# Input laid out feature-major by the host, row norms as column sums of squares, first weights in four loads

## The chip, the cores and the metric

The kernel runs on one core of a Trainium2 chip. The metric is the device time of one execution in microseconds (us), as the median of several runs. A core has a matrix engine (TensorE, in the profile PE for matmuls and PEld for weight loads), a vector engine (VectorE, DVE), an activation engine (ScalarE, ACT), a general engine (GpSimd, POOL) and SyncE (SP), which here only issues DMAs. Each engine works through its own instructions in order and waits on semaphores for the others. DMAs are issued from SP's queue and, a few, from ACT's.

## The reference

Two layers of a diffusion trunk: 512 latent tokens and 256 context tokens of width 1024, all in float32. Layer 0 is differential attention, layer 1 grouped-query attention. Only the beginning of layer 0 matters here:

```python
def rms_norm(x, g):
    y = xf * lax.rsqrt(jnp.mean(xf * xf, axis=-1, keepdims=True) + NORM_EPS)
    return (y * g).astype(x.dtype)
...
    shift, scale, gate = split(silu(c) @ ada_w[i] + ada_b[i], 3)
    cshift, cscale, cgate = split(silu(c_ctx) @ ada_w[i] + ada_b[i], 3)
    h  = rms_norm(x,  pre_g[i]) * (1.0 + scale)  + shift
    hc = rms_norm(xc, pre_g[i]) * (1.0 + cscale) + cshift
    p = h @ a_w_in        # q, k, v, z; the same weights for hc
```

So h, the input of the first projections, needs the norm of each token's row and a shift and a scale for each of 1024 features. The shift and scale weights of layer 0 are 1024 x 2048 floats, 8.4 MB, for two vectors c and c_ctx.

## The kernel before

Everything is kept feature-major: a tile of 128 features (feature tile kt, 0 to 7) lies on the 128 partitions and the tokens lie along the free dimension, 512 latent ones and then 256 context ones (768). A float32 product is made of three float32r matmuls: each operand is split in a high part (`whi`, `h` from a cast on ACT) and a low part (`wlo`, the second `h`, from a subtraction on DVE or POOL), and `mm3` (lines 146 to 148) multiplies high by high, high by low and low by high.

The opening stage of layer 0, the first 50 us or so, does this:

- `x_load` (L551) brings the tokens in six tiles of 128 tokens x 1024 features, rows of 4 KB, four of x first and two of the context later.
- `x_tile` squares each tile on ACT with a sum (L571), makes 1/norm on POOL (`rstd_of`, L382 and L383), scales the tile (L217, on DVE, one on POOL), transposes it on PE in eight 128x128 pieces (L577) and copies the result to `xnt`, 128 features x 8 x 768 tokens (L582 on ACT, L584 on DVE).
- `ada_load8` (L489) and `ada_load` (L475) bring the shift/scale weights as they lie in the layer's matrix: feature tiles 0 and 1 each as a first small group in runs of 512 bytes, then three groups of two feature tiles in runs of 1 KB. I number these five groups first to fifth. `ada_pe` multiplies them with silu(c) in four column strips (`cols4`, L465), `ada_red` copies the row to SBUF (L496), turns it into columns (L500) and adds the biases (`mods_set`, L510 to L512): `mods` holds shift and scale.
- `ht` makes h for one feature tile, latent or context: hf = xnt * scale + shift (L602), cast (L603), low part (L604).
- `w_load` and `v_load` (L527, L532) bring the first head's q and k weights in two halves and its v weights in two tiles; `w_split` and `v_split` (L539 to L545) split them.
- `qk_part` and `v_part` are the projections by `mm3`: q and k of head 0 into `sc`, v of heads 0 and 1 into the `bk` banks, feature tile by feature tile as h becomes available.

The code is written once, in program order with priorities (`tc.high_priority`, offsets in `PRI`); a scheduler puts the instructions of each engine in order ahead of the run from its own model of the time. The tables `EXS`, `EHF`, `EHL`, `EWL`, `EVL` choose DVE ('v'), POOL ('p') or ACT ('a') for single steps. The DMAs of one queue start in the order written; a DMA waits, on SP, for its buffer and for the DMA eight places before it.

```python
    row = pj(256)
    run(ada_pe(ca, row))
    w_split(0, raw_qk)
    row_b = pj(256)
    ada_red(0, 1, row)
    run(ada_pe(cb, row_b))
    ht(0, 0)
```

Of the kernel before, what the change touches and what calls it, by code (L numbers as in the profile page):

```python
# [9 lines left out]
F32 = mybir.dt.float32  # L10
F32R = mybir.dt.float32r
AF = mybir.ActivationFunctionType
ALU = mybir.AluOpType
# [3 lines left out]
P = 128  # L17
D = 1024
KT = 8
S = 512  # L20
C = 256
T = 768
NT = 6
NQ = 4
# [14 lines left out]
AGB = 11  # L39
# [9 lines left out]
XE = [2, 2, 2, 2, 3, 3]  # L49
NWARM = 12  # L50
XLATE = 1
# [28 lines left out]
def f32(ap):  # L80
    return ap.bitcast(F32)
# [3 lines left out]
def tile_backbone(  # L85
    ctx: ExitStack,
    tc: tile.TileContext,
    x: bass.AP,
    xc: bass.AP,
    c_col: bass.AP,  # L90
    ada_w: bass.AP,
    ada_bT: bass.AP,
# [13 lines left out]
    nc = tc.nc  # L106
    uid = [0]

    def nm(s):
        uid[0] += 1  # L110
        return f"{s}_{uid[0]}"
# [8 lines left out]
    def small(n=1):  # L120
        return sm.tile([P, 8], F32, tag="sm", name=nm("sm"), bufs=24)[:, :n]
# [5 lines left out]
    def trp():  # L127
        i = lru.pop(0)
        lru.append(i)
        return banks[i]  # L130
# [10 lines left out]
    def sc2():  # L141
        scs.append(scs.pop(0))
        return scs[-1]
# [17 lines left out]
    eps = con.tile([P, 1], F32, name="eps")  # L161
# [5 lines left out]
        nc.tensor.matmul(banks[3][:, :P], ones, ones, start=True, stop=True)  # L167

    ccol = con.tile([P, 2, KT], F32, name="ccol")
    nc.sync.dma_start(ccol, c_col)  # L170
# [42 lines left out]
    def scaled(eng, dst, src, s_):  # L213
        if eng == "a":
            nc.scalar.activation(dst, src, AF.Copy, scale=s_)
        else:
            (nc.vector if eng == "v" else nc.gpsimd).tensor_scalar(dst, src, s_, 1.0, ALU.mult, ALU.mult)  # L217

    VP = {"v": nc.vector, "p": nc.gpsimd}
# [215 lines left out]
    hhi, hlo = [None] * KT, [None] * KT  # L435
# [29 lines left out]
                prev = nc.tensor.matmul(  # L465
                    o[32 * j:32 * j + 32, :], s32[:, 4 * g + j, :], ts[j], start=g == 0, stop=g == 1)

    ada_v = ada_w[0].rearrange("(k p) (w n) -> p k w n", p=P, w=3)
# [14 lines left out]

    def ada_load8(e):
        cs = []
        for k in (0, 4):
            g = st.tile([P, D], F32, tag="ag", name=nm("ag"), bufs=AGB).rearrange("p (k w n) -> p k w n", k=4, w=2)
            for w in range(2):
                nc.sync.dma_start(g[:, :, w], ada_v[:, k:k + 4, w, e * P:(e + 1) * P])  # L489
            cs += [g[:, j].rearrange("p w n -> p (w n)") for j in range(4)]  # L490
        return cs

    def ada_red(k0, nb, o):
# [20 lines left out]
    def raw_tile():  # L514
        return wp.tile([P, 1024], F32, tag="raw", name=nm("raw"), bufs=2)
# [4 lines left out]
    del ws.items[:4]  # L520
    ws.pools.append(ws.pools.pop(0))

    def w_load(half):
        r = raw_tile()
        sl = slice(half * 512, half * 512 + 512)
        for j in range(2):
            nc.sync.dma_start(r[:, j * 512:j * 512 + 512], a_w[j][:, sl])  # L527
        return r

    def v_load(half):  # L530
        rv = raw_tile()
        nc.sync.dma_start(rv, a_w[half * 4 + 2])  # L532
        return rv

    def w_split(half, r):
        sl = slice(half * 512, half * 512 + 512)
        for j, (hi, lo) in enumerate((wq, wk0)):
            rj = r[:, j * 512:j * 512 + 512]
            nc.scalar.copy(hi[:, sl], rj)  # L539
            VP[EWL[2 * half + j]].tensor_tensor(lo[:, sl], rj, f32(hi[:, sl]), ALU.subtract)  # L540

    def v_split(half, rv):
        hi, lo = wv0[half]
        nc.scalar.copy(hi, rv)
        VP[EVL[half]].tensor_tensor(lo, rv, f32(hi), ALU.subtract)  # L545

    xs = []

    def x_load(t):
        xt = st.tile([P, D], F32, tag="ag", name=nm("xt"), bufs=AGB)  # L550
        nc.sync.dma_start(xt, x[t * P:(t + 1) * P, :] if t < NQ else xc[(t - NQ) * P:(t - NQ + 1) * P, :])  # L551
        xs.append(xt)

    for t in range(NQ):
        x_load(t)
    ca = ada_load8(0)
    raw_qk = w_load(0)
    cb = ada_load8(1)
    raw_v = v_load(0)
    if XLATE < 1:  # L560
        x_load(4)
        x_load(5)
    nxt = ada_load(1)
    if XLATE:
        x_load(4)
        x_load(5)

    def x_tile(t):
        ssq = small()
        junk = st.tile([P, D], mybir.dt.bfloat16, tag="junk", name=nm("junk"), bufs=1)  # L570
        nc.scalar.activation(junk, xs[t], AF.Square, accum_out=ssq)  # L571
        r = rstd_of(ssq, D)
        scaled(EXS[t], xs[t], xs[t], r)
        pt = [sc2()] if t < NQ else [trp(), trp()]
        for kt in range(KT):
            o = pt[0][:, kt // 4, :] if t < NQ else pt[kt // 4]
            nc.tensor.transpose(o[:, (kt % 4) * P:(kt % 4 + 1) * P], xs[t][:, kt * P:(kt + 1) * P], ident)  # L577
        for j in range(2):
            src = (pt[0][:, j] if t < NQ else pt[j]).rearrange("p (k n) -> p k n", k=4)
            dst = xnt[:, 4 * j:4 * j + 4, t * P:(t + 1) * P]  # L580
            if XE[t] >> j & 1:
                nc.scalar.copy(dst, src)  # L582
            else:
                nc.vector.tensor_copy(dst, src)  # L584

    def pri(f, i):
        def g(*args):
            with tc.high_priority(offset=PRI[i]):
                f(*args)

        return g

    def ht(kt, v):
        if v == 0:
            hhi[kt], hlo[kt] = htile(), htile()
        a, b = ((0, 512), (512, 768))[v]
        hf = st.tile([P, 512], F32, tag="hf", name=nm("hf"), bufs=2)[:, :b - a]
        s_, h_ = mods[:, 0, v, 1, kt:kt + 1], mods[:, 0, v, 0, kt:kt + 1]
        if EHF[v][kt] == "a":
            nc.scalar.activation(hf, xnt[:, kt, a:b], AF.Identity, scale=s_, bias=h_)  # L600
        else:
            VP[EHF[v][kt]].tensor_scalar(hf, xnt[:, kt, a:b], s_, h_, ALU.mult, ALU.add)  # L602
        nc.scalar.copy(hhi[kt][:, a:b], hf)  # L603
        VP[EHL[v][kt]].tensor_tensor(hlo[kt][:, a:b], hf, f32(hhi[kt][:, a:b]), ALU.subtract)  # L604

    x_tile, ht, ada_red, w_split, v_split = pri(x_tile, 0), pri(ht, 1), pri(ada_red, 2), pri(w_split, 3), pri(v_split, 3)
    for t in range(NQ):
        x_tile(t)
    row = pj(256)
    run(ada_pe(ca, row))  # L610
    w_split(0, raw_qk)
    row_b = pj(256)
    ada_red(0, 1, row)
    run(ada_pe(cb, row_b))
# [43 lines left out]
    run(qk_part((0,), 0))  # L658
    ada_red(1, 1, row_b)
    ht(1, 0)  # L660
    v_split(0, raw_v)
    raw_qk = w_load(1)
    raw_v = v_load(1)
    ov = [pj(512) for _ in range(2)]
    for pr in range(NQT):
        kts = (2 * pr, 2 * pr + 1)
        if pr + 1 < NQT:
            cs = nxt
            if pr + 2 < NQT:
                nxt = ada_load(pr + 2)  # L670
            row = pj(512)
            ada = ada_pe(cs, row)
            if pr == 0:
                mix(ada, qk_part((1,), 0), v_part(kts, (0, 1, 2, 3)))
            else:
                mix(ada, qk_part(kts, 0), v_part(kts, (0, 1)))
            ada_red(2 * pr + 2, 2, row)
            if pr == 0:
                w_split(1, raw_qk)
            if pr == 1:  # L680
                v_split(1, raw_v)
# [920 lines left out]
    return ra, rb.reshape(P, 2, 512)  # L1602


# [57 lines left out]
```

## Time and profile before

| | |
|---|---|
| time, three runs | 838.15, 838.4, 839.8 us; median 838.4 |
| profiled execution | span 840.2 us from its first to its last instruction, the time that the profile gives for it |
| TensorE busy | 801.7 us of the span; 30.6 of the first 40 us |
| DMA | 77.78 MB over the span; 15.95 MB of it in the first 60 us |
| granted TensorE clock | 0.990 on average |

The profile is one execution; its span lies 1.8 us above the median of the runs. Rows of instructions give the start, the duration, the engine, the line of the kernel, the operation, what it writes and reads and its shape; in brackets stands how long the engine was idle before it and what ended that. Rows of groups give a count, the busy time, the mean duration in ns, and the idle time before with its releasers. An f32 matmul that isn't float32r shows as two records.

### The profile page before, as it was taken

The numbers are of one execution on the slowest core, as the hardware profiler recorded it, in microseconds if no ns is written. First come the engines' busy times: TensorE is split into PE (matmuls) and PEld (weight loads), VectorE is DVE, ScalarE is ACT, GpSimd is POOL, SyncE is SP. The second block draws the span as 40 slices with busy tenths as digits, with TensorE's granted clock in tenths as the row PEclk, the third lists the DMA queues.
The fourth block names the chain that finished last, engine by engine and source line by source line (L and its number), as shares of the span: only waits on it lengthen the run. The fifth ranks groups of instructions, "written<-read, shape, count | busy, mean of one in ns | idle before, by whom it ended". The sixth has DMA issues, their size and how long they took to land. (4 is left out here: it accounts for less than half of the span.)

```text
span 840.2 us, 14479 instructions
## 1 busy us (share of the span) xinstructions
PE 801.7 (95%) x5472; PEld 705.9 (84%) x5472; DVE 477.9 (57%) x897; ACT 459.0 (55%) x1001; POOL 452.8 (54%) x629
## 2 busy tenths in 40 slices
PE   7899999999999999999999999989998989899997
PEld 5578888888877898778988898779998889889986
DVE  4424467764858425675267843664266676665634
ACT  5424457664574644765457743754364656566731
POOL 4344676966476753776733312585776746624201
PEclk9999999999999999999999999999999999999999
DMA  9934211122133321314410051031232340300112
GB/s 300 352 109 126 88 39 35 67 83 82 63 114 116 122 77 63 137 52 151 126 51 26 27 200 51 26 108 51 77 101 76 86 162 4 101 26 26 53 48 101
DMA packets 41541, 77.78 MB, mean 93 GB/s; under 512 B 3584, under 2 KB 18688, under 8 KB 41472
## 3 DMA queue, kind: packets, MB, share of 16 engines
q1 hardware_dynamic: 38048, 71.71, 26.0%
q10 hardware_dynamic: 3424, 5.15, 1.8%
q8 instruction: 43, 0.70, 0.3%
q14 instruction: 26, 0.21, 0.1%
HBM read 70.56 MB, written 2.10 MB: 86 GB/s over the span
## 5 line engine op out<-in xcount | busy, mean ns | idle before, releaser
L146 PE MATMUL bk<-whi,h 128*128 128x256 f32 (+1 forms) x592 | 176.7, 301 | 6.5 <-ACT hf L1229 2.0
L203 POOL TENSOR_TENSOR wlo<-raw,whi 128x256 fp32r<-128x256 f32 x184 | 138.6, 784 | 70.3 <-ACT whi L209 69.3
L147 PE MATMUL bk<-wlo,h 128*128 128x256 f32 (+1 forms) x592 | 175.8, 298 | 0.3 <-DVE wlo L203 0.3
L148 PE MATMUL bk<-whi,h 128*128 128x256 f32 (+1 forms) x592 | 174.8, 298 | 0.8 <-DVE h L1232 0.8
L146 PE MATMUL bk<-h,whi 128*128 128x512 f32 (+2 forms) x416 | 147.1, 354 | 3.1 <-ACT sq L968 1.5
L147 PE MATMUL bk<-h,whi 128*128 128x512 f32 (+2 forms) x416 | 144.7, 348 | 0.0
L148 PE MATMUL bk<-h,wlo 128*128 128x512 f32 (+2 forms) x416 | 144.7, 348 | 0.1
L146 PEld LDWEIGHTS bk<-whi,h 128*128 128x128 f32 x592 | 112.0, 189 | 15.8 <-issue 3.6
L147 PEld LDWEIGHTS bk<-wlo,h 128*128 128x128 f32 x592 | 112.2, 189 | 4.8 <-issue 1.0
L148 PEld LDWEIGHTS bk<-whi,h 128*128 128x128 f32 x592 | 111.6, 189 | 4.8 <-DVE h L1232 1.2
L217 POOL TENSOR_SCALAR p<-p,sm 128x768 f32<-128x768 f32 (+1 forms) x80 | 67.7, 849 | 76.6 <-DVE sm L882 29.1
L146 PEld LDWEIGHTS bk<-h,whi 128*128 128x128 f32 x416 | 78.2, 188 | 17.8 <-issue 4.8
L209 ACT CAST whi<-raw 128x1024 fp32r<-128x1024 f32 x64 | 67.4, 1053 | 39.2 <-DMA raw<-in_b_w 12.3
L148 PEld LDWEIGHTS bk<-h,wlo 128*128 128x128 f32 x416 | 78.1, 188 | 8.6 <-issue 1.3
L147 PEld LDWEIGHTS bk<-h,whi 128*128 128x128 f32 x416 | 78.3, 188 | 6.5 <-issue 0.3
L879 ACT ACTIVATE p<-sc,sm 128x768 f32<-128x768 f32 (+1 forms) x68 | 59.9, 883 | 25.8 <-DVE sm L876 25.1
L876 DVE TENSOR_REDUCE sm<-sc 128x1 f32<-128x768 f32 (+1 forms) x68 | 60.6, 918 | 20.5 <-PE sc L871 20.5
L203 POOL TENSOR_TENSOR sz<-sz,za 128x192 f32<-128x192 f32 (+1 forms) x48 | 32.5, 697 | 41.2 <-ACT za L183 41.2
L939 ACT CAST ah<-bk 128x512 fp32r<-128x512 f32 x56 | 31.7, 592 | 34.4 <-PE bk L936 28.1
L887 DVE SCALAR_TENSOR_TENSOR p<-p,sm,p 128x768 f32<-128x768 f32 (+1 forms) x34 | 38.4, 1129 | 20.2 <-POOL p L217 19.0
L940 DVE TENSOR_TENSOR al<-bk,ah 128x512 fp32r<-128x512 f32 x56 | 37.6, 685 | 17.4 <-ACT ah L939 16.9
L871 PE MATMUL sc<-qk,qk 64*128 64x384 f32 (+1 forms) x396 | 46.8, 359 | 0.1
(247 smaller groups left out, 1720.2 us busy)
## 6 DMA issues: line engine op xcount, KB each, us to landing
raw<-in_a_w SPq DMA_DIRECT2D x30, 512.0 KB, 3.5
araw<-in_ada_w SPq DMA_DIRECT2D x12, 1024.0 KB, 5.1
raw<-in_b_w SPq DMA_DIRECT2D x20, 512.0 KB, 3.5
ag<-in_ada_w SPq DMA_DIRECT2D x32, 256.0 KB, 6.4
raw<-in_w_out SPq DMA_DIRECT2D x16, 512.0 KB, 3.4
sw<-qr ACTq DMA_DIRECT2D x32, 128.0 KB, 2.4
raw<-in_ada_w SPq DMA_DIRECT2D x8, 512.0 KB, 3.9
xt<-in_x SPq DMA_DIRECT2D x4, 512.0 KB, 5.4
```

Source lines behind the costliest of these rows:

```text
L146: nc.tensor.matmul(o, ahi, bhi, start=start, stop=False)
L147: nc.tensor.matmul(o, ahi, blo, start=False, stop=False)
L148: nc.tensor.matmul(o, alo, bhi, start=False, stop=stop)
L203: eng.tensor_tensor(dst[:, i:i + n], a[:, i:i + n], b[:, i:i + n], op)
L209: nc.scalar.copy(hi, r)
L217: (nc.vector if eng == "v" else nc.gpsimd).tensor_scalar(dst, src, s_, 1.0, ALU.mult, ALU.mult)
L871: prev = nc.tensor.matmul(sc[m][:, j if nk == T else m, :w], a[r, tok], b[r, c], start=i == 0, stop=i == 2)
L876: nc.vector.tensor_reduce(mx, scv, AX.XY if nk == T else AX.X, ALU.max, negate=True)
L879: nc.scalar.activation(pv_, scv, AF.Exp, bias=mx, accum_out=l[:, m:m + 1])
L887: nc.vector.scalar_tensor_tensor(ps_[0], pt, r, ps_[0], ALU.mult, ALU.add)
L939: nc.scalar.copy(ah, tr)
L940: nc.vector.tensor_tensor(al, tr, f32(ah), ALU.subtract)
```

## The change

The host now gives x and the context transposed (`xlT`, `xcT`: 128 x 8 x tokens), and the shift/scale weights of layer 0 in the order in which they are loaded (`ada0`, 16 tiles of 128 x 1024), so that each partition's part of a load is one run of 4 KB. The tokens go straight into `xnt`. The row norms are no longer taken from token-major tiles: `x_norm` squares `xnt` on ACT, adds pairs on DVE, and a matmul with a matrix of ones sums over the features and spreads the sum over all partitions; Ln and Exp on ACT give 1/norm for each token along the free dimension (`rsb`). `ht` multiplies by scale and by `rsb` in one DVE operation, adds the shift on ACT while casting, and forms the low part in one DVE operation with the shift as scalar; all of this is on DVE and ACT, nothing on POOL. The first weights come in four loads of three DMAs, each with the q, k and v parts for two feature tiles; the first is split on DVE, the others on POOL in pieces of 256 columns. The load of the conditioning vector goes from SP's queue to ACT's. The priorities change.

```diff
-EWL = 'pppp'
-EVL = 'pp'
-PRI = (-100, 0, 400, 0)
+EWL = 'vppp'
+PRI = (1500, 300, 400, 0)
...
-    nc.sync.dma_start(ccol, c_col)
+    nc.scalar.dma_start(ccol, c_col)
...
     def ada_load(qt):
         cs = []
-        for k in range(0, KT, 2):
-            g = st.tile([P, D], F32, tag="ag", name=nm("ag"), bufs=AGB).rearrange("p (k w n) -> p k w n", k=2, w=2)
-            for j in range(2):
-                nc.sync.dma_start(g[:, j], ada_v[:, k + j, 0:2, qt * 256:qt * 256 + 256])
-            cs += [g[:, j].rearrange("p w n -> p (w n)") for j in range(2)]
+        for k in range(4):
+            g = st.tile([P, D], F32, tag="ag", name=nm("ag"), bufs=AGB)
+            nc.sync.dma_start(g, ada0[4 * qt + k])
+            cs += [g[:, j * 512:j * 512 + 512] for j in range(2)]
         return cs
...
     def ada_load8(e):
         cs = []
-        for k in (0, 4):
-            g = st.tile([P, D], F32, tag="ag", name=nm("ag"), bufs=AGB).rearrange("p (k w n) -> p k w n", k=4, w=2)
-            for w in range(2):
-                nc.sync.dma_start(g[:, :, w], ada_v[:, k:k + 4, w, e * P:(e + 1) * P])
...
+        for k in range(2):
+            g = st.tile([P, D], F32, tag="ag", name=nm("ag"), bufs=AGB)
+            nc.sync.dma_start(g, ada0[2 * e + k])
+            cs += [g[:, j * 256:j * 256 + 256] for j in range(4)]
...
+    def w_load(q):
         r = raw_tile()
         for j in range(2):
+            nc.sync.dma_start(r[:, j * 256:j * 256 + 256], a_w[j][:, q * 256:q * 256 + 256])
+        nc.sync.dma_start(r[:, 512:], a_w[q // 2 * 4 + 2][:, q % 2 * 512:q % 2 * 512 + 512])
         return r
+    def w_split(q, r):
+        parts = [(wq, q * 256, 0, 256), (wk0, q * 256, 256, 256), (wv0[q // 2], q % 2 * 512, 512, 512)]
+        for (hi, lo), c, a, n in parts:
+            nc.scalar.copy(hi[:, c:c + n], r[:, a:a + n])
+            pieces(VP[EWL[q]], lo[:, c:c + n], r[:, a:a + n], f32(hi[:, c:c + n]), ALU.subtract)
+    def x_load(v, c):
+        if v == 0:
+            nc.sync.dma_start(xnt[:, 2 * c:2 * c + 2, :S], xlT[:, 2 * c:2 * c + 2, :])
+        else:
+            nc.sync.dma_start(xnt[:, 4 * c:4 * c + 4, S:], xcT[:, 4 * c:4 * c + 4, :])
+
+    for c in range(4):
+        x_load(0, c)
     ca = ada_load8(0)
-    raw_qk = w_load(0)
+    raw_w = [w_load(0)]
     cb = ada_load8(1)
-    raw_v = v_load(0)
+    raw_w.append(w_load(1))
     nxt = ada_load(1)
...
+    x_load(1, 0)
+    x_load(1, 1)
...
+    rsb = st.tile([P, T], F32, name="rsb")
+    def x_norm(v):
+        n = (S, C)[v]
+        per = 1024 // n
+        a, b = ((0, S), (S, T))[v]
+        o = trp()[:, :n]
+        for c in range(KT // per):
+            sq = st.tile([P, 1024], F32, tag="sqx", name=nm("sqx"), bufs=2)
+            nc.scalar.activation(sq.rearrange("p (k n) -> p k n", k=per), xnt[:, c * per:c * per + per, a:b], AF.Square)
+            nc.vector.tensor_tensor(sq[:, :512], sq[:, :512], sq[:, 512:], ALU.add)
+            if v:
+                nc.vector.tensor_tensor(sq[:, :n], sq[:, :n], sq[:, n:512], ALU.add)
+            nc.tensor.matmul(o, ones, sq[:, :n], start=c == 0, stop=c == KT // per - 1)
+        nc.scalar.activation(rsb[:, a:b], o, AF.Ln, scale=1.0 / D, bias=eps)
+        nc.scalar.activation(rsb[:, a:b], rsb[:, a:b], AF.Exp, scale=-0.5)
...
     def ht(kt, v):
...
-            VP[EHF[v][kt]].tensor_scalar(hf, xnt[:, kt, a:b], s_, h_, ALU.mult, ALU.add)
-        nc.scalar.copy(hhi[kt][:, a:b], hf)
-        VP[EHL[v][kt]].tensor_tensor(hlo[kt][:, a:b], hf, f32(hhi[kt][:, a:b]), ALU.subtract)
+        nc.vector.scalar_tensor_tensor(hf, xnt[:, kt, a:b], s_, rsb[:, a:b], ALU.mult, ALU.mult)
+        nc.scalar.activation(hhi[kt][:, a:b], hf, AF.Identity, bias=h_)
+        nc.vector.scalar_tensor_tensor(hlo[kt][:, a:b], hf, h_, f32(hhi[kt][:, a:b]), ALU.add, ALU.subtract)
...
-    for t in range(NQ):
-        x_tile(t)
+    x_norm(0)
...
             if pr == 0:
                 for kt in (2, 3):
                     ht(kt, 0)
-                x_tile(4)
-                x_tile(5)
+                x_norm(1)
                 for kt in range(4):
                     ht(kt, 1)
```

The scheduler puts PE's instructions in another order around the projections of feature tile 1. On PE before, after tile 0's first products come those of tile 1 (`h_299` and `h_300`), and only then the first half of the third shift/scale group (`ag_172`, `ag_169`):

```order
L146 MATMUL sc_72<-h_299,whi_136 128x512
L146 MATMUL sc_73<-h_299,whi_138 128x512
L147 MATMUL sc_72<-h_300,whi_136 128x512
L148 MATMUL sc_72<-h_299,wlo_137 128x512
L147 MATMUL sc_73<-h_300,whi_138 128x512
L148 MATMUL sc_73<-h_299,wlo_139 128x512
L465 MATMUL bk_69<-ag_172,s_127 32x512 x2
L465 MATMUL bk_69<-ag_169,s_127 32x512 x2
L147 MATMUL bk_68<-wlo_141,h_280 128x256
```

On PE after, at the same place, tile 1's products (`h_241`) come behind the reduction of the second group and the whole of the third (`ag_164` to `ag_170`):

```order
L150 MATMUL bk_71<-whi_140,h_223 128x256
L498 MATMUL bk_68<-sel_130,row_234 128x2 x2
L467 MATMUL bk_70<-ag_166,s_127 32x512 x2
L467 MATMUL bk_70<-ag_164,s_127 32x512 x2
L467 MATMUL bk_70<-ag_170,s_127 32x512 x2
L467 MATMUL bk_70<-ag_168,s_127 32x512 x2
L148 MATMUL sc_72<-h_241,whi_136 128x512
L148 MATMUL sc_73<-h_241,whi_138 128x512
L148 MATMUL bk_69<-whi_140,h_241 128x256
```

The third group moved ahead of tile 1's projections, so that on PE tile 1 now stands behind the loads of that group.

On ACT before, the way to the first h (`h_280`) leads over the squares of the four x tiles and four copies of transposed tiles, with the casts of the first weights between them:

```order
L571 ACTIVATE junk_237,sm_236<-xt_150 128x1024
L582 COPY xnt<-sc_72 128x4x128
L582 COPY xnt<-sc_73 128x4x128
L539 CAST whi_136<-raw_158 128x512
L582 COPY xnt<-sc_72 128x4x128
L539 CAST whi_138<-raw_158 128x512
L496 COPY row_265<-bk_68 128x256
L582 COPY xnt<-sc_73 128x4x128
L603 CAST h_280<-hf_282 128x512
```

On ACT after, the way to the first h (`h_222`) leads over the four squares, Ln (L564) and Exp (L565), with two casts and a row copy between these two:

```order
L183 ACTIVATE ta<-ta 128x16
L559 ACTIVATE sqx_183<-xnt 128x1024
L185 ACTIVATE ta<-ta 128x16
L559 ACTIVATE sqx_187<-xnt 128x1024
L564 ACTIVATE rsb<-bk_68,eps 128x512
L531 CAST whi_136<-raw_152 128x256
L494 COPY row_207<-bk_69 128x256
L531 CAST whi_138<-raw_152 128x256
L565 ACTIVATE rsb<-rsb 128x512
L531 CAST whi_140<-raw_152 128x512
L581 ACTIVATE h_222<-hf_224,mods 128x512
```

The copies of transposed tiles are gone from ACT, and the silu steps of the conditioning vector (`ta`) have moved between the squares.

More of the change, by code (lines that the diff above doesn't have):

```diff
@@ L89, in tile_backbone @@
     xc: bass.AP,
+    xlT: bass.AP,
+    xcT: bass.AP,
+    ada0: bass.AP,
     c_col: bass.AP,
@@ L521, in tile_backbone @@
     ws.pools.append(ws.pools.pop(0))
-    def w_load(half):
+    def w_load(q):
         r = raw_tile()
-        sl = slice(half * 512, half * 512 + 512)
         for j in range(2):
-            nc.sync.dma_start(r[:, j * 512:j * 512 + 512], a_w[j][:, sl])
-        return r
[L530 to L552, printed above, removed]
-    for t in range(NQ):
-        x_load(t)
+            nc.sync.dma_start(r[:, j * 256:j * 256 + 256], a_w[j][:, q * 256:q * 256 + 256])
@@ L556, in tile_backbone @@
+    for c in range(4):
+        x_load(0, c)
     ca = ada_load8(0)
-    raw_qk = w_load(0)
+    raw_w = [w_load(0)]
     cb = ada_load8(1)
-    raw_v = v_load(0)
-    if XLATE < 1:
-        x_load(4)
-        x_load(5)
+    raw_w.append(w_load(1))
     nxt = ada_load(1)
[L564 to L584, printed above, removed]
+    x_load(1, 0)
@@ L598, in ht @@
         s_, h_ = mods[:, 0, v, 1, kt:kt + 1], mods[:, 0, v, 0, kt:kt + 1]
[L599 to L607, printed above, removed]
-        x_tile(t)
+        nc.vector.scalar_tensor_tensor(hf, xnt[:, kt, a:b], s_, rsb[:, a:b], ALU.mult, ALU.mult)
+        nc.scalar.activation(hhi[kt][:, a:b], hf, AF.Identity, bias=h_)
+        nc.vector.scalar_tensor_tensor(hlo[kt][:, a:b], hf, h_, f32(hhi[kt][:, a:b]), ALU.add, ALU.subtract)
+    x_norm, ht, ada_red, w_split = pri(x_norm, 0), pri(ht, 1), pri(ada_red, 2), pri(w_split, 3)
+    x_norm(0)
     row = pj(256)
     run(ada_pe(ca, row))
-    w_split(0, raw_qk)
+    w_split(0, raw_w[0])
     row_b = pj(256)
@@ L660, in tile_backbone @@
     ht(1, 0)
-    v_split(0, raw_v)
-    raw_qk = w_load(1)
-    raw_v = v_load(1)
+    w_split(1, raw_w[1])
+    raw_w.append(w_load(2))
+    raw_w.append(w_load(3))
     ov = [pj(512) for _ in range(2)]
@@ L1602, in _tables, with _ada0 @@
     return ra, rb.reshape(P, 2, 512)
+def _ada0(w):
+    import numpy as np
+    v = w.reshape(KT, P, 3, D)[:, :, :2].transpose(1, 0, 2, 3)
+    res = np.empty((16, P, 1024), np.float32)
+    for e in range(2):
+        for k in range(2):
+            res[2 * e + k] = v[:, 4 * k:4 * k + 4, :, e * P:(e + 1) * P].reshape(P, 1024)
+    for q in range(1, 4):
+        for k in range(4):
+            res[4 * q + k] = v[:, 2 * k:2 * k + 2, :, q * 256:(q + 1) * 256].reshape(P, 1024)
+    return res
 def kernel(**inputs):
@@ L1636 @@
         "xc": cc(g["ctx"][0]),
+        "xlT": cc(cols(g["x"][0]).swapaxes(1, 2)),
+        "xcT": cc(cols(g["ctx"][0]).swapaxes(1, 2)),
+        "ada0": _ada0(g["ada_w"][0]),
         "c_col": cc(cols(np.stack([g["c"][0], g["c_ctx"]]))),
```

7 lines of the change are left out of this document (2 added, 5 removed).

## Prediction

> **What bounds the kernel now.** I read the totals first, then engine time by stage (first 50 us in steps of ten), then TensorE's waits in the first 65 us, then the instructions of that stage in order of time.
>
> ```profile
> PE 801.7 (95%) x5472; PEld 705.9 (84%) x5472; DVE 477.9 (57%) x897; ACT 459.0 (55%) x1001; POOL 452.8 (54%) x629
> ```
> ```profile
> 0.00:10.00 10.00, 6.58 (x32) 6.05 (x32) 1.97 (x12) 6.30 (x12) 3.66 (x12) 1.00 0.77 266
> 10.00:20.00 10.00, 8.09 (x66) 5.42 (x66) 6.07 (x12) 5.56 (x12) 4.78 (x6) 0.83 1.15 328
> 20.00:30.00 10.00, 7.43 (x38) 5.00 (x39) 4.10 (x6) 2.08 (x4) 3.11 (x3) 0.83 1.08 365
> 30.00:40.00 10.00, 8.45 (x72) 6.55 (x71) 4.72 (x10) 6.58 (x13) 3.83 (x5) 1.00 0.99 333
> 40.00:50.00 10.00, 10.00 (x76) 8.06 (x69) 5.16 (x14) 3.27 (x7) 6.39 (x7) 1.00 0.73 249
> 50.00:110.00 60.00, 59.93 (x365) 47.84 (x364) 24.09 (x38) 20.71 (x37) 31.61 (x39) 1.00 0.26 84
> 110.00:160.00 50.00, 47.92 (x326) 40.67 (x325) 34.42 (x62) 33.64 (x72) 37.46 (x49) 1.00 0.16 53
> ```
> In a row of the second table stand the stretch, its length, the busy time of PE, weight loads, DVE, ACT and POOL, the granted clock, the DMA share and GB/s. The change touches only the first 50 us. There PE is idle for 9.4 us of 40, runs at a reduced clock in the second and third row, and the DMA share is at or near 1. From 40 to 110 us PE never stops: what arrives earlier at 40 us arrives earlier at 110.
>
> ```profile
> PE sc L146 <- ACT h L603: 3.3, 2, 2.6
> PE sc L577 <- POOL xt L217: 2.2, 1, 2.2
> PE bk L500 <- ACT row L496: 1.7, 2, 0.8
> ...
> PE bk L146 <- ACT h L603: 0.7, 1, 0.7
> ```
> The longest waits are for h, the modulated input, and then for row norms and shift/scale rows.
>
> ```profile
> GB/s 0 98 271 403 426 365 308 299 357 301 293 364 358 349 352 356 397 390 354 355 372 354 348 360 320 249 337 382 359 347 92 55 298 14 0 0 0 93 257 0
> ```
> That is DMA traffic over the first 60 us in slices of 1.5 us: 403 and 426 while x comes in rows of 4 KB, about 300 where the first shift/scale weights come in runs of 512 B, about 355 where they come in runs of 1 KB.
>
> ```profile
> 0.72 0.37 SPq L170 DMA_DIRECT2D ccol<-in_c_col  x1
> 1.15 1.91 SPq L551 DMA_DIRECT2D xt<-in_x  x4
> 5.36 1.06 ACT L571 ACTIVATE junk<-xt 128x1024 bf16<-128x1024 f32 x1 [1.87 <-DMA xt<-in_x]
> 19.14 0.72 PE L146 MATMUL sc<-h,whi 128*128 128x512 f32 x2 [0.69 <-ACT h L603]
> 20.38 2.37 POOL L545 TENSOR_TENSOR wlo<-raw,whi 128x1024 fp32r<-128x1024 f32 x1 [2.55 <-ACT whi L544]
> 20.43 2.33 DVE L512 TENSOR_TENSOR mods<-mods,pre 128x2 f32<-128x2 f32 x1
> 24.05 1.22 PE L146 MATMUL sc<-h,whi 128*128 128x512 f32 x2 [2.57 <-ACT h L603]
> ...
> 46.83 0.39 PE L146 MATMUL sc<-h,whi 128*128 128x512 f32 x1
> ...
> 48.23 0.28 PE L146 MATMUL sc<-h,whi 128*128 128x256 f32 x1
> ...
> 49.63 0.28 PE L146 MATMUL bk<-whi,h 128*128 128x256 f32 x1
> ```
> Tile 0's projections start at 19.14, tile 1's at 24.05; the latent q and k of tiles 2 and 3 end at 48.23. I call that point M: up to it both programs do the same projections, behind it PE has the same work left. The forecast is M after against 48.23.
>
> **The change part by part.** Durations I use:
>
> ```profile
> 1.04 5.49 PE L167 MATMUL bk<-ones 128*128 128x128 f32 x24 [1.04 <-DVE mhalf L164]
> 8.70 1.09 PE L577 MATMUL sc<-ident,xt 128*128 128x128 f32 x8 [2.18 <-POOL xt L217]
> 15.35 0.64 PE L465 MATMUL bk<-ag,s 128*32 128x256 f32 x8
> 17.65 0.20 DVE L512 TENSOR_TENSOR mods<-mods,pre 128x2 f32<-128x2 f32 x1
> 19.70 0.50 PE L500 MATMUL bk<-sel,row 128*128 128x2 f32 x4
> 39.42 1.07 PE L465 MATMUL bk<-ag,s 128*32 128x512 f32 x8
> 45.47 0.95 PE L500 MATMUL bk<-sel,row 128*128 128x2 f32 x8
> L496 ACT COPY row<-bk 128x512 f32<-128x512 f32 x3 | 1.8, 589 | 10.6 <-PE bk L465 10.6
> L496 ACT COPY row<-bk 128x256 f32<-128x256 f32 x2 | 0.7, 372 | 0.0
> L603 ACT CAST h<-hf 128x512 fp32r<-128x512 f32 x6 | 3.7, 623 | 9.2 <-DVE hf L602 9.2
> L604 DVE TENSOR_TENSOR h<-hf,h 128x512 fp32r<-128x512 f32 x8 | 5.5, 691 | 3.7 <-ACT h L603 3.7
> L1179 DVE TENSOR_TENSOR u<-bk,gate 128x256 f32<-128x256 f32 x8 | 3.1, 420 | 7.6 <-PE bk L148 7.6
> L1208 DVE SCALAR_TENSOR_TENSOR x<-u,sm,x 128x512 f32<-128x512 f32 x8 | 5.7, 748 | 1.9 <-POOL sm L393 1.7
> L203 POOL TENSOR_TENSOR wlo<-raw,whi 128x256 fp32r<-128x256 f32 x184 | 138.6, 784 | 70.3 <-ACT whi L209 69.3
> ```
> PE's pitch from start to start stands in the rows at M: six matmuls of 512 columns from 46.83 to 48.23 (0.233 each), twelve of 256 from there to 49.63 (0.117 each).
>
> Loads. ccol goes to ACT's queue, whose first computation waits until 5.36 anyway, so its issue costs nothing; x moves up by 1.15 - 0.72 = 0.43 us, so its first tile is there at 4.93. From it to the last tile of the third shift/scale group (feature tiles 2 and 3) 13 tiles of 512 KB follow: three of x, two and two of the first groups, one and one of weights, four of the third. In runs of 4 KB a tile takes 0.524 MB / 415 GB/s = 1.26 us; I take 1.3, and 0.4 us more in all for the weights, now cut to 1 and 2 KB runs: 4.93 + 16.9 + 0.4 = 22.2. At 355 GB/s, the rate of the 1 KB runs, a tile takes 1.48 and the end is 24.5. [...]
>
> Norms. Out go six squares with sums, the POOL power, six scalings of x, 48 transposes (8 take 1.09) and their copies. In come four squares of 1.06, four DVE adds of 0.69 and four matmuls against ones, 512 wide in f32. No such matmul is in the trace; the warm-up ones, 12 of 128 columns in 5.49 us (two records each), give 0.46 per 128, so 1.83 for 512 as the upper end; 128 columns of a transpose take 0.14, so the lower end is 0.55. I take 0.92, an estimate at half the upper end, since PE has been running for 5 us by then, and carry 1.83 along. The chain: last x tile 4.93 + 3.9 = 8.8; its square, behind ACT's earlier ones and four small silu steps, 9.3 to 10.4; add to 11.1; matmul to 12.0 or 12.9; Ln 0.6, two casts and a row copy of 0.38 queued behind it, Exp 0.6: 14.3 to 15.2; hf 0.75 and h 0.62: 15.7 to 16.6; six hand-overs of 0.1: PE starts tile 0 at 16.3 to 17.2, not 19.14. That is no gain yet: tile 0's twelve matmuls (2.1, or 4.2 should the clock be halved), a group of 0.64 and a row reduction of 0.5 end at 20 to 22.5, and PE's order then has the whole third group before tile 1. So tile 1 starts at 22.2 + 1.07 = 23.3, against 24.05, and PE has already done what it did later before.
>
> From there to M by PE's order: tile 1 q, k 6 x 0.233 = 1.40; v of tiles 0 and 1, 18 x 0.117 = 2.11; reduction 0.95; two ones-matmuls of 256, 0.92; fourth group 2.14; v of tiles 2 and 3, 24 x 0.117 = 2.81; context q, k, v of tiles 0 and 1, 2.81; reduction 0.95; tiles 2 and 3 q, k 12 x 0.233 = 2.80. Sum 16.9. Before, the same stretch also held the third group (2.14), four more v matmuls (0.47) and 16 transposes (2.18), without the ones: 20.7, done in 48.23 - 24.05 = 24.2, so 3.5 were lost to waits and the reduced clock. After, I allow 1.2: 0.5 for the fourth group, which reuses the bank that Ln reads, and 0.7, the last wait for h listed above. M comes at 23.3 + 16.9 + 1.2 = 41.4, **6.8 us earlier**. Ends: no waits and 415 GB/s give 8.5; 355 GB/s and all 3.5 of the waits give 2.2.
>
> Engines beside. DVE now makes every h: per pair of feature tiles four operations of 0.75 and four of 256 columns, about 0.42 each, 4.7 us where PE needs some 10; covered. It also splits the first weight load, three pieces, one of which (0.69) sits between hf and the low part of h, under the wait for the third group. ACT casts in twelve smaller pieces instead of six, about 1 us more, in its idle time (20.5 of 40 us busy). POOL loses the norms, the h parts and the 1024-wide subtractions; its 12 pieces of 0.784 are 9.4, where it had two of 2.37 and four of half their size, about the same. The later loads: from 22.2, some 13 tiles to the end of the fifth group, about 40; PE needs the first of it at 44.
>
> Behind M. 59.93 of 60 us busy says that nothing waits to 110 us, and the order of instructions from about the third head on is the same as before; between, it is reshuffled, where 2.1 us are idle (the row from 110 to 160): plus or minus 1.2 in the range.
>
> The profiled execution's span is 840.2, 1.8 above the median of 838.4; I make the sum in the span, 833.4, and give 838.4 - 6.8 = **831.6**.
>
> **Rivals.** *The waits come back.* For it: red-to-h chains (three mods steps, 0.5 in all, hf 0.75, h 0.62) sit only just under PE's cover, and the rows with the reduced clock (0.83) are those with idle stretches. Against: the third group now runs before tile 1, so that its chain lies beside 2 us of v. All 3.5 lost again: gain 4.5, 833.9.
>
> *The loads are no faster,* the change of layout not doing what it says. For it: 355 GB/s held for most of the first 45 us. Against: 403 and 426 with 4 KB runs. Tile 1 at 25.6, gain 4.5, 833.9.
>
> *Slower: DVE blocked by POOL.* The rows at 20.38 and 20.43 show a DVE step on 128x2 that lasts until POOL's subtraction is over, 2.33 us instead of the 0.20 at 17.65. After, every h takes two DVE operations with two SBUF inputs. If each of POOL's 12 pieces stood once in the path to PE, 12 x 0.784 = 9.4 are lost: 831.6 + 9.4 = 841.0. It decides from 11 pieces on (6.8 + 1.7 = 8.5 us). Against: the pieces come in three bursts, two of which lie after 33 us, when h is well ahead. [...]
>
> *Given back.* The reshuffled heads or several small losses eat 5 us: 836.7 or a little above.
>
> **How the numbers follow.** This kernel's runs lie 0.2% apart, so 0.2% (1.7 us) is about what a measurement can tell from no change. Chances: forecast 0.57, waits back 0.21, slow loads 0.10, given back to within 0.2% 0.07, slower 0.05. The first three are faster: 0.88. The range goes from 829.0 (8.5 and 1.2 behind M would be 828.7) to 836.0 (2.2 is 836.2); outside lie the last two cases and the tips, 0.18.
>
> **What would show it.** Right: tile 0's first L148 near 16.5, the third group's last L467 near 23, tile 1 right behind it, the transposes gone, M at 41 to 42, GB/s near 400 from 5 to 20 us, and the whole difference there by 50 us. Wrong: PE waits for h or for rsb of a microsecond or more after 24 us; DVE operations of 1.5 us beside POOL's pieces; a third group after 24; or M early and the end not.

## The result and the profile after

The changed kernel takes 830.45 us in the median of four runs (829.79 to 832.4), against 839.1 for the kernel before in the same comparison. The ratio is 0.9878 with a 95% interval of 0.9846 to 0.9911. A second comparison gave 0.9898 (0.9868 to 0.9928). On the 838.4 us of the kernel before these are 828.2 and 829.8: 8.6 to 10.2 us faster, where 6.8 were forecast. Below, "after" in microseconds stands for 0.9888, the middle of the two, 9.4 us.

The first lines are the totals and the engine time by stage of the profiled execution after (span 828.4 us, columns as before: PE, weight loads, DVE, ACT, POOL, granted clock, DMA share, GB/s).

```profile
PE 794.2 (96%) x5436; PEld 700.7 (85%) x5436; DVE 483.8 (58%) x909; ACT 456.6 (55%) x997; POOL 435.5 (53%) x612
```
```profile
0.00:10.00 10.00, 7.86 (x29) 6.02 (x30) 3.45 (x14) 5.63 (x9) 0.69 (x6) 1.00 0.82 283
10.00:20.00 10.00, 7.81 (x48) 3.56 (x48) 3.94 (x9) 5.25 (x12) 3.06 (x4) 0.83 1.04 399
20.00:30.00 10.00, 9.16 (x62) 6.24 (x60) 5.44 (x14) 3.93 (x7) 0.00 (x0) 1.00 1.05 390
30.00:40.00 10.00, 10.00 (x77) 7.98 (x78) 8.36 (x17) 5.73 (x12) 3.33 (x4) 1.00 0.98 363
40.00:50.00 10.00, 10.00 (x66) 7.28 (x64) 5.39 (x11) 2.96 (x7) 3.40 (x4) 1.00 0.35 106
50.00:110.00 60.00, 59.39 (x382) 51.29 (x379) 32.55 (x53) 25.82 (x47) 34.06 (x44) 1.00 0.29 97
110.00:160.00 50.00, 47.47 (x328) 41.18 (x327) 33.77 (x58) 32.95 (x74) 36.09 (x48) 0.97 0.13 43
```

PE idles for 5.2 us of the first 40 instead of 9.4, and only one of the four stages there has a reduced clock. From 50 to 160 PE is no busier than before: 106.9 us here, 107.9 there. TensorE's longest waits in the first 65 us, and the DMA traffic over the first 60 in slices of 1.5 us:

```profile
PE sc L148 <- ACT h L581: 1.3, 1, 1.3
PE bk L563 <- DVE sqx L560: 1.1, 3, 0.4
...
PE bk L498 <- ACT row L494: 0.8, 1, 0.8
```
```profile
GB/s 0 138 308 390 358 422 418 374 407 397 387 412 401 412 363 348 389 408 415 401 391 383 402 386 375 393 101 183 167 0 0 44 298 8 0 0 33 309 19 0
```

One wait for h is left where there were several. From 4.5 to 39 us the traffic holds between 348 and 422 GB/s, against about 300 and 355 before. In order of time:

```profile
4.90 1.06 ACT L559 ACTIVATE sqx<-xnt 128x1024 f32<-128x1024 f32 x1 [2.90 <-DMA xnt<-in_xlT]
11.36 1.13 PE L563 MATMUL bk<-sqx,ones 128*128 128x512 f32 x2
16.50 1.22 PE L148 MATMUL sc<-h,whi 128*128 128x512 f32 x2 [1.34 <-ACT h L581]
21.31 2.17 PE L467 MATMUL bk<-ag,s 128*32 128x512 f32 x16
22.41 0.16 PEld L467 LDWEIGHTS bk<-ag,s 128*32 128x32 f32 x8 [0.95 <-DMA ag<-in_ada]
23.41 0.73 PE L148 MATMUL sc<-h,whi 128*128 128x512 f32 x2
...
41.64 0.28 PE L148 MATMUL sc<-h,whi 128*128 128x256 f32 x1
```

x is there at 4.90, the norm's last matmul starts at 11.36, tile 0 at 16.50, the third shift/scale group runs from 21.31 with its last load landing at 22.4, tile 1 follows at 23.41, and M, the first context product, is at 41.64: 6.6 us before the 48.23 of the other profile. So in this execution everything up to M came as forecast. When each PE instruction is set beside the same one before, the lead is 6.6 at M, 8.9 at 56 us, 7.5 from 156 to 200, 7.7 at 300, 9.7 at 500 and 12.1 at 780; the spans differ by 11.8. What the forecast has no term for begins between M and 56 us.

The fifth shift/scale group lies there. PE before, then PE after (an f32 matmul counts twice in the xcount, so x2 is one strip of 32 columns):

```profile
51.37 1.04 PE L465 MATMUL bk<-ag,s 128*32 128x512 f32 x2
...
53.01 1.06 PE L465 MATMUL bk<-ag,s 128*32 128x512 f32 x6
...
55.95 1.05 PE L465 MATMUL bk<-ag,s 128*32 128x512 f32 x4
...
58.16 1.05 PE L465 MATMUL bk<-ag,s 128*32 128x512 f32 x4
```
```profile
45.48 1.06 PE L467 MATMUL bk<-ag,s 128*32 128x512 f32 x8
...
49.24 1.06 PE L467 MATMUL bk<-ag,s 128*32 128x512 f32 x8
```

The same eight strips are four runs before (1, 3, 2 and 2) and two runs of four after, and every run lasts 1.04 to 1.06 us, whether it holds one strip or four. The four strips of a run start 7 ns apart. The start-to-start times around a run add to this: after the first run of before, 0.98 us pass to the next projection, and the projections on either side of a run come at a pitch of 0.32 to 0.34 instead of 0.23, so a run costs about 0.98 + 0.19 = 1.17 us. Two runs fewer are 2.3 us, the step from 6.6 to 8.9. PE does not idle in this stretch in either profile, and the projections in it are the same in number and shape.

### The profile page after: what moved, and what is told of

It reads as the page before. It is cut to its first block, busy times and chain, and to the rows that moved or that the text cites. A ratio compares the mean times of both kernels' runs of the same rounds, so it can differ in the third digit from the quotient of the medians.

```text
span 828.4 us, 14363 instructions
## 1 busy us (share of the span) xinstructions
PE 794.2 (96%) x5436; PEld 700.7 (85%) x5436; DVE 483.8 (58%) x909; ACT 456.6 (55%) x997; POOL 435.5 (53%) x612
## 5 line engine op out<-in xcount | busy, mean ns | idle before, releaser
L205 POOL TENSOR_TENSOR wlo<-raw,whi 128x256 fp32r<-128x256 f32 x196 | 148.4, 788 | 117.9 <-ACT whi L211 82.0
L862 DVE SCALAR_TENSOR_TENSOR p<-p,sm,p 128x768 f32<-128x768 f32 (+1 forms) x34 | 39.0, 1146 | 24.3 <-POOL p L219 23.5
L914 ACT CAST ah<-bk 128x512 fp32r<-128x512 f32 x56 | 31.8, 590 | 31.6 <-PE bk L911 27.3
L915 DVE TENSOR_TENSOR al<-bk,ah 128x512 fp32r<-128x512 f32 x56 | 37.5, 684 | 17.5 <-ACT ah L914 17.3
```

The source lines that it names most:

```text
L205: eng.tensor_tensor(dst[:, i:i + n], a[:, i:i + n], b[:, i:i + n], op)
L862: nc.vector.scalar_tensor_tensor(ps_[0], pt, r, ps_[0], ALU.mult, ALU.add)
L914: nc.scalar.copy(ah, tr)
L915: nc.vector.tensor_tensor(al, tr, f32(ah), ALU.subtract)
```

## The experiments

Each was timed in five rounds beside the kernel before, and its ratio is to that kernel. A difference between two variants is a difference of two such ratios, each uncertain by 1.4 to 2.7 us, so differences of 1 to 3 us are read from the traces.

**The fifth group side by side, in the kernel before.**

```diff
-            cols4(o, g, cs[4 * g:4 * g + 4])
+            with tc.high_priority(offset=300 if adj else 0):
+                cols4(o, g, cs[4 * g:4 * g + 4])
```

`adj` is true for the fifth group alone.

> The kernel before, with the strip matmuls of the fifth shift/scale group kept side by side on PE: two runs of four instead of runs of 1, 3, 2 and 2 between projections. Theory S (a run of strips costs PE about 1.16 us whatever its length, 0.98 for the strips and 0.19 for the slower pitch around them, because the four strips start 7 ns apart and run at the same time): two runs fewer, 2.3 us faster, 836.5 to 837. Theory H (the extra gain behind M comes from waits and order in the later heads, or is the scatter of single profiles; strips cost by their count): no change, 838.4 to 839.5.

Ratio 0.9969 (0.9950 to 0.9988), 2.6 us faster (1.0 to 4.2). The trace has the two runs:

```profile
49.98 1.06 PE L465 MATMUL bk<-ag,s 128*32 128x512 f32 x8
53.89 1.07 PE L465 MATMUL bk<-ag,s 128*32 128x512 f32 x8
```

Set beside the trace of before, PE is 2.4 us earlier at 64 to 70 us. This edit too reshuffled the heads behind, and from 200 to 400 us 0.8 of it is left; so the strips are shown by the trace at 64 us, and that the runs differ by about as much in the end is in part chance.

**The same strips one by one, in the kernel after.**

```diff
-            cols4(o, g, cs[4 * g:4 * g + 4])
-            yield
+            for j in (3, 2, 1, 0) if scat else (0,):
+                if scat:
+                    with after(lastmm[0]):
+                        lastmm[0] = nc.tensor.matmul(
...
+                yield
```

`scat` is true for the fifth group alone, whose strips `mix` now puts one behind each of the first eight projection steps.

> The kernel after, with the eight strip matmuls of the fifth group put one by one between projections, eight runs of one instead of two of four. Theory S: six more runs at 1.16 us, 7.0 us slower than after, about 837.4. Theory H (strips cost by their count): as after, 830.5 plus or minus 0.8.

Ratio to before 0.9974 (0.9957 to 0.9990), so 7.2 us slower than after. Eight runs of one:

```profile
45.77 1.05 PE L485 MATMUL bk<-ag,s 128*32 128x512 f32 x2
47.17 1.04 PE L485 MATMUL bk<-ag,s 128*32 128x512 f32 x2
```

Set beside the trace of after, PE is 8.2 us late at 64 us: 7.0 for the runs, 0.7 behind a wait for h that the late row causes, and 0.5 that were there at M, where this execution had a longer stretch of reduced clock. At 240 us it is 8.1 late. A delay made at 50 us is thus carried one to one where the order behind it stays; that part of the forecast held. Theory S stands in both directions.

**The layout alone, in the kernel before** (`ada_load8` and `ada_load` read `ada0`, 4 KB runs).

> The kernel before with only the shift/scale weights of layer 0 in load order, 4 KB a partition; x and norms, h and first weights as before, and the fifth group still in four runs. Theory L (the loads carry the gain): the third group lands about 4 us earlier, and with tile 0 still held to about 19 us by the norms, M moves by 2 to 4 us: 835 to 837. Theory X (the norms and the way to the first h carry it): under 1 us, 838 to 839.

Ratio 1.0048 (1.0030 to 1.0065): 4 us slower, which neither theory had.

```profile
20.13 2.32 DVE L509 TENSOR_TENSOR mods<-mods,pre 128x2 f32<-128x2 f32 x1
23.74 0.94 PE L147 MATMUL sc<-h,whi 128*128 128x512 f32 x2 [2.57 <-ACT h L600]
...
26.47 1.56 PE L466 MATMUL bk<-ag,s 128*32 128x512 f32 x8
...
35.87 1.97 PE L574 MATMUL bk<-ident,xt 128*128 128x128 f32 x8 [2.21 <-DVE xt L218]
```

The third group's last load lands at 23.5 us instead of 26.3. But tile 1 starts only 0.3 us earlier than before and the third group 0.4, because tile 1 is still held by DVE's step of 2.32 us beside POOL's subtraction. Then PE waits 2.2 us for the transposes of the context tiles, and runs at half clock for 6.8 us from 34.3 on. The context tiles themselves are not late: the first lands at 26.1 instead of 27.5. What is late is ACT's square of it, which the scheduler now puts behind the row copy of the third group (ACT before, then ACT here):

```profile
27.56 1.06 ACT L571 ACTIVATE junk<-xt 128x1024 bf16<-128x1024 f32 x1 [3.56 <-DMA xt<-in_xc]
```
```profile
31.96 0.59 ACT L493 COPY row<-bk 128x512 f32<-128x512 f32 x1 [8.28 <-PE bk L466]
32.44 1.06 ACT L568 ACTIVATE junk<-xt 128x1024 bf16<-128x1024 f32 x1
```

Up to 33 us the faster loads buy next to nothing here; the 4 us are lost behind, by this trace through the order on ACT. No run undoes that order alone.

**The layout undone, in the kernel after** (shift/scale loads from `ada_w` in 512 byte and 1 KB runs).

> The kernel after with the shift/scale weights brought from the layer's matrix as before (runs of 512 bytes and 1 KB, twice as many DMAs); x feature-major, norms by ones, first weights in four loads as after. Theory L: the third group lands at 24.5 to 26 us instead of about 22, tile 1 waits for it, M 2.5 to 4 us later: 833 to 834.5. Theory X: under 1 us, 830 to 831.5.

Ratio 0.9937 (0.9913 to 0.9961), 4.1 us slower than after.

```profile
22.14 1.06 PE L467 MATMUL bk<-ag,s 128*32 128x512 f32 x8 [0.58 <-DMA ag<-in_ada_w]
25.16 1.06 PE L467 MATMUL bk<-ag,s 128*32 128x512 f32 x8 [1.96 <-DMA ag<-in_ada_w]
26.15 1.04 PE L148 MATMUL sc<-h,whi 128*128 128x512 f32 x2
```

PE waits for the third group to 25.16 and tile 1 comes at 26.15, 2.7 us later than after; PE is 3.6 late at 33 us, in part by a stretch of reduced clock at 26.4 behind these waits, and 3.7 at 154. Here the layout carries 3 to 4 us.

**After once more**, unchanged.

> The kernel after, unchanged, against more runs of the kernel before. Theory S (6.8 us up to M as forecast, and 2.3 us from two fewer runs of strips behind M): 9.1 us, ratio 0.989. Theory F (the forecast as it stood, the rest of the first comparison being scatter): 6.8 us, ratio 0.992. Theory H (the centre of the first comparison, with waits or order in the later heads): 10.2 us or more, ratio 0.988 or less. In its trace, against the first profile of this kernel, what differs shows what one execution scatters by.

Ratio 0.9898 (0.9868 to 0.9928). Theory S's 0.989 lies in both intervals. So does the forecast's 0.992 in this one, at its upper end, but not in the first. In the trace of this second execution M is at 43.81, 2.2 us later than in the first: tile 0 still starts at 16.43, but the clock is reduced for 10.2 us from 15.7 us on instead of for 3.4. Behind 33 us the two executions keep that distance to the end.

**The third group loaded earlier, in the kernel after.**

```diff
+    nxt = ada_load(1)
     raw_w.append(w_load(1))
-    nxt = ada_load(1)
```

> The kernel after with the second load of first weights (0.52 MB) moved behind the third shift/scale group, so that this group lands about 1.3 us earlier; the fifth group's strips kept in two runs of four, as in after. Theory P (PE and the landing reach the second half of the third group at the same moment, 22.4; PE lost only 0.1 us to the landing): tile 1 starts at 23.2 to 23.4, time as after within 0.5 us. Theory G (the landing alone sets tile 1, as the forecast's sum has it): tile 1 at about 22.1, 1.3 us faster than after.

Ratio 0.9950 (0.9927 to 0.9973): 5 us slower than after.

```profile
19.88 2.04 PE L467 MATMUL bk<-ag,s 128*32 128x512 f32 x16
22.63 0.74 PE L148 MATMUL sc<-h,whi 128*128 128x512 f32 x2 [0.72 <-ACT h L582]
```

The third group no longer waits for its load, and tile 1 then waits 0.72 for h: 0.8 earlier than after, between the two expectations, in a stage that this execution ran at full clock, where after had one reduced stretch. By 42 us PE is 0.2 behind after. The loss comes later: the scheduler reshuffled the heads that follow, and TensorE's waits from 44 to 185 us grew from 3.0 to 7.5 us in sum, the longest for p:

```profile
PE bk L912 <- DVE p L863: 3.7, 3, 1.6
PE bk L148 <- DVE vlo L784: 1.6, 1, 1.6
PE sc L847 <- ACT p L855: 1.4, 1, 1.4
```

At 182 us PE is 6.7 us behind. An edit in the first 20 us can cost more by the order that it leaves behind than it wins where it was made.

**The ones matmul in one pass, in the kernel after** (sums stored as float32r, `ones_r`).

> The kernel after with the squares' sums stored as float32r, so that the ones matmul is one pass; loads as in after; fifth group in two runs. The scheduler now puts only half of the third group ahead of tile 1. Theory P: tile 0's first product 0.8 to 1.2 us earlier than 16.5, and tile 1, no longer behind the whole third group, at 21.5 to 22.5; M 0.5 to 1.5 us earlier. Theory G: tile 0 earlier, but what was won is lost again in front of the third group's second half (lands at 22.4); M and the time as after within 0.5 us.

Ratio 0.9921 (0.9898 to 0.9944), 2.8 us slower than after. The first two ones matmuls, one record each where after has two, took 0.50 instead of 1.13, but the scheduler put both halves of the second group ahead of tile 0, and the clock was reduced from 8.6 to 18.9 us (in after from 16.3 to 19.8), where the last two took 0.80. Tile 0 came at 17.67 instead of 16.50, tile 1 at 22.92. How much of this is the order and how much the clock isn't shown; the next run has the same order and the same stretch. At 41 us PE is 0.6 us behind after, at 176 us 3.4, lost in the heads again. Both theories missed tile 0.

**Both together.**

> Both: third group loaded ahead of the second load of first weights, and the ones matmul in one pass; the whole third group stands ahead of tile 1 again; fifth group in one run of strips. Theory P: landing and PE's chain both move by about 1 us, tile 1 at 22.2 to 22.5, 1 us faster than after. Theory G: 1.3 us, the same as with the earlier load alone.

Ratio 0.9885 (0.9855 to 0.9916), the same as after. Tile 1 at 23.00. With the order changed at three places and the clock reduced from 8.8 to 19.1 us, this tells neither theory from the other.

**POOL's first v subtractions in pieces, in the kernel before** (with the fifth group in two runs).

```diff
-        VP[EVL[half]].tensor_tensor(lo, rv, f32(hi), ALU.subtract)
+        pieces(VP[EVL[half]], lo, rv, f32(hi), ALU.subtract)
```

> The kernel before with the fifth group's strips in two runs of four, and with POOL's subtractions for the first v weights in four pieces of 256 columns instead of one of 1024 (2.37 us), beside which DVE's last step of the second group's shift/scale took 2.33 us. Theory K (that step held tile 1): it takes under 1 us, tile 1's way to h is 1.5 to 2 us shorter, PE works through v of tile 0 meanwhile, M 1 to 2 us earlier than 48.2; time 1 to 2 us under that of before with two runs alone (ratio 0.997), so 0.995. Rival (the third group, landing at 26, is waited for next): M and time as with two runs alone, 0.997.

Ratio 0.9929 (0.9907 to 0.9952): 3.4 us on top of the strips, 6.0 in all.

```profile
20.82 0.74 POOL L203 TENSOR_TENSOR wlo<-raw,whi 128x256 fp32r<-128x256 f32 x1 [2.55 <-ACT whi L545]
20.88 0.69 DVE L513 TENSOR_TENSOR mods<-mods,pre 128x2 f32<-128x2 f32 x1
...
23.24 0.73 PE L146 MATMUL sc<-h,whi 128*128 128x512 f32 x2 [0.85 <-ACT h L604]
```

DVE's step now ends with the first piece, 0.69 instead of 2.33 us, PE has put six v matmuls ahead of tile 1 instead of two, and from 28 to 50 us it is 2.5 to 3.3 us earlier than with two runs alone, and 3.3 at 240. Theory K holds, with more than it expected: 3.4 against 1 to 2. Tile 1 is 0.8 us earlier and four v matmuls (0.5) are done besides; the rest goes with the reduced-clock stretch at 24 us behind the 2.57 us wait for h, which is gone with that wait.

**All first splits on POOL and unsplit, in the kernel after.**

> The kernel after with all splits of the first weights on POOL and unsplit (256 and 512 columns as they come); the fifth group falls into three runs of strips (1, 3, 4) instead of two. Theory S for the strips: 1.2 us. Theory K (DVE's two-input steps wait for POOL's subtraction): hf of tile 0 stands beside three subtractions of 0.8, 0.8 and about 1.2 us, tile 0 comes 1 to 2 us later than 16.5, M 0.5 to 1.5 us later; together 832.2 to 833.5. Without K: 831.7, tile 0 at 16.5 or earlier since DVE has three steps less.

Ratio 0.9887 (0.9866 to 0.9907): no difference that shows beside an interval of 1.7 us either way, where 1.2 to 3 us were expected.

```profile
15.10 0.75 DVE L580 SCALAR_TENSOR_TENSOR hf<-xnt,mods,rsb 128x512 f32<-128x512 f32 x1
15.17 2.95 POOL L532 TENSOR_TENSOR wlo<-raw,whi 128x512 fp32r<-128x512 f32 x2 [0.19 <-ACT whi L531]
16.66 0.84 PE L148 MATMUL sc<-h,whi 128*128 128x512 f32 x2 [1.68 <-ACT h L581]
```

DVE's step began 0.07 before POOL's and took its usual 0.75, and tile 0 is 0.16 late. In this pair and in the pair at 20.4 before, whichever started first went through; the DVE step that was held there, 2.33 us instead of 0.20, began 0.05 behind a POOL one of 2.37. The third run of strips did cost its 1.2 us at 47. By 131 us PE is level with after, whose reduced-clock stretch at 126 is missing here, but by 156 it is 1.3 us behind again; the spans differ by 0.8.

**Layout, pieces and strips in the kernel before**, transposes and norms as they were.

> The kernel before with three edits together: shift/scale weights in load order, POOL's first v subtractions in pieces of 256, the strips of the fifth group side by side; x token-major with transposes as before. Theory A (the layout adds its 3 to 4 us to any order in which tile 1 is not held on DVE): 3 to 4 us under before_pc, ratio 0.988 to 0.990, as fast as after without the new norms. Theory B (the layout pays only with x feature-major; the context tiles, which need the buffers of the shift/scale loads, come late as in the layout alone, and PE waits for their transposes): ratio 0.993 to 1.000.

Ratio 0.9952 (0.9934 to 0.9970), not faster than without the layout. The number is Theory B's: the context tiles' transposes start at 34.2 and 38.5 and PE waits 1.8 us for h at 33, a time that without the layout transposes fill from 31.33 on. Its cause is not what the trace shows. The first context tile lands at 25.8, earlier than the 28.4 without the layout, and its square on ACT starts at 30.16 instead of 28.43, behind the row copy, as in the layout alone. So by both traces it is the order on ACT that eats the gain of the loads. What the layout would be worth with token-major x and the old order isn't shown.

## Why the forecast was right and wrong

**Up to M it was right by its own steps, with some luck in the last digit.** x at 4.90 (4.93 forecast), ones matmuls at a pitch of 1.06 (0.92), tile 0 at 16.50 (16.3 to 17.2), third group landed at 22.4 (22.2), tile 1 at 23.41 (23.3), M at 41.64 (41.4). The 13 tiles took 17.5 us where the sum had 17.3, which is 390 GB/s over all and 408 in the third group alone. The second execution, with M at 43.81 by its reduced clock, shows that a hit within 0.3 us is partly luck.

**The step that failed is "Behind M".** It said that behind M "PE has the same work left", took over the 6.8 us without a term for the order, and allowed plus or minus 1.2 for the reshuffled heads. The work is the same by count, but it has not the same price in another order: two runs of strips fewer are 2.3 us. Both directions were run: 2.4 us by 64 us for two runs fewer (2.6 in the time), 7.0 by 53 us for six more (7.2 in the time). With it the forecast would have been 838.4 - 6.8 - 2.3 = 829.3, ratio 0.989, which lies in both intervals. The rest of the way to the end is not closed: the lead of 8.9 us falls to 7.5 by 156 us and rises again behind 300. The rows that told it were at hand: the runs of strips stand in the order of both programs, and the prediction's own row at 39.42 shows eight records in 1.07 us, four strips side by side. In that run too the four strips start 7 ns apart, and where a projection stands between two strips, as in the eight runs of one, the next strip pays in full, 1.04 to 1.05 us.

**The bound of 1.2 us for the heads was too narrow.** Between before and after the lead changes there by 1.4, from 8.9 to 7.5, with a reduced-clock stretch at 126 us in the profile after; the earlier load and the one-pass norm lost 6.5 and 2.9 us there, though at 41 us they are only 0.2 and 0.6 behind after.

**Where the 6.6 us at M come from was only half seen.** The forecast named layout and norms. The same stretch held a DVE step blocked by POOL on the way to tile 1, and removing it is worth 3.4 us to the kernel before, the reduced clock behind it included. The prediction quoted that pair of rows, and used it only as a way to be slower. It had been a cost of the kernel before: the wait stands in the 24.05 at which tile 1 starts, and the reduced clock behind it, from 23.9 to 27.3 us, in the "3.5 were lost to waits and the reduced clock". The layout gives nothing in the kernel before, with the order that the scheduler makes of it, and 4.1 us in the kernel after. New norms and h without the layout (0.9937) equal strips and pieces in the old kernel (0.9929), so no gain of their own is shown for them. The four weight loads and the priorities were not tried by themselves.

**The rivals.** Waits did not come back: one wait for h of 1.3 us. The loads were faster. DVE beside POOL's pieces at 38 us took 2.07 for two hf steps instead of 1.41, under cover.

**The span against the median.** Of the 11.8 us between the two profiles some 2 to 3 are taken to be one execution's scatter, not the change. The lead grows from 8.3 at 400 us to 9.7 and then 12.1, behind the stretches of reduced clock at 437 and 730 us that only the execution before has. The first looks like chance: the kernel before with its strips side by side has none there, and the kernel after with all splits on POOL has one. For the second this isn't shown.

## What to carry to other kernels

Before a shift is called "carried one to one", go through the order behind it for instructions whose price depends on their neighbours: here the strips of a tiled matmul cost about 1.17 us for each run, of one strip or of four, so keep them side by side. When a row shows an engine blocked on the path to the bottleneck, price its removal first, by the smallest edit; here splitting one POOL instruction and grouping eight matmuls gave the kernel before 6.0 us (4.0 to 7.8), against 9.4 for the whole change. And a single-part experiment in a scheduled kernel is read from its trace, up to the point where the order differs: look first whether another engine's order, here ACT's, has moved.

## What the runs showed of the hardware

The stretches of reduced clock are 3.41 us long, or two or three of that (6.8 us from 34.3 on in the layout alone, 10.2 from 15.7 on in after once more), and each of the five behind 100 us in the two profiles (apart from those at the very end) follows a wait of TensorE. In the kernel before, in stretches that long, around 730 us:

```profile
727.00:730.40 3.40, 1.39 (x10) 0.97 (x9) 2.52 (x4) 3.37 (x7) 2.77 (x4) 1.00 0.50 157
730.40:733.80 3.40, 3.16 (x12) 3.06 (x13) 2.29 (x4) 2.69 (x7) 1.54 (x2) 0.51 0.47 154
```
```profile
730.64 0.69 PE L146 MATMUL sc<-kh,qh 128*128 128x384 f32 x1 [2.25 <-ACT p L1414]
```

PE waited 2.25 us, and then ran 3.4 us at half clock (0.51 in that row); a matmul of 384 columns took 0.69 us in it, 0.34 before the wait, so the 3.16 us of matmuls in it cost about another 1.6. The profile after has the same instruction at 719.98 with a wait of 1.55 and no such stretch. The others before, at 437 and 638, follow waits of 1.6 and 2.5 us; those after, at 126 and 627, follow 1.4 and 3.1. So five waits of 1.4 to 3.1 us were followed by such a stretch, and one of 1.55 was not. The same program differs in this from run to run: the second profile of after is 2.2 us longer than the first (830.6, 828.4), with three such stretches around 16 to 26 us instead of one:

```profile
10.00:20.00 10.00, 7.80 (x47) 3.58 (x46) 3.94 (x9) 5.24 (x12) 3.06 (x4) 0.79 1.04 398
20.00:30.00 10.00, 10.00 (x54) 6.44 (x52) 3.95 (x9) 3.23 (x5) 0.00 (x0) 0.70 1.05 390
```

About 1.1 us for each stretch, which is also the order of the scatter between runs of one kernel.

The traces show what goes with it. In each of the two profiles the stretches start whole multiples of 3.413 us apart: before at 10.24, 23.89, 436.90, 638.29 and 730.45 us, 4, 125, 184 and 211 of them behind the first; after at 16.34, 125.57 and 627.33, 32 and 179 of them. Cut into pieces of 3.413 us, counted from these starts and without their last 8 us, the two profiles have 7 pieces at full clock in which TensorE was busy for less than half, and each was followed by one at half clock; of 12 pieces that were busy for 50 to 70%, one was (before, the piece from 433.49 us, busy for 1.84 us); of 452 busier ones, none. So in these two profiles, up to there, every wait that left such a piece less than half busy was followed by a reduced stretch; in the last 8 us before has one, from 832.85 us, that was busy for 48% and was not. Where the pieces lie differs between executions of one kernel: in after the reduced clock of the opening stage starts at 16.34 us in the first profile and at about 15.7 in the second.
